# Turning the feed-forward hidden blocks with 32x32 transposes on VectorE and DMAs, in place of 128x128 transposes on TensorE

## The chip, the cores and the metric

The kernel runs on one core of a Trainium2 chip. The metric is device time in microseconds (us) for one execution; smaller is better. The core's engines run side by side and wait for one another through semaphores: TensorE (PE; its weight loads are shown apart as PEld), VectorE (DVE), ScalarE (ACT), GpSimd (POOL) and SyncE (SP), which issues nearly all DMAs. An "engine queue" below is the fixed order in which one engine takes its instructions: what stands behind a waiting instruction waits too.

## What is computed

One encoder layer on a sequence of 256 tokens of width 2048, all in float32: a feed-forward half step, a mixer (a gated linear recurrence beside a windowed attention), and a second feed-forward half step, each closed by a layer norm. Only the two feed-forward steps are touched by the change:

```python
def swiglu(x, w_in, w_out):
    gate, up = jnp.split(x @ w_in, 2, axis=-1)
    return (jax.nn.silu(gate) * up) @ w_out
...
h = layer_norm(DEEPNORM_ALPHA * h + 0.5 * swiglu(h, ffn1_w_in[layer], ffn1_w_out[layer]), ...)
mix = hybrid_mixer(h, ...)
h = layer_norm(DEEPNORM_ALPHA * h + mix, ...)
h = layer_norm(DEEPNORM_ALPHA * h + 0.5 * swiglu(h, ffn2_w_in[layer], ffn2_w_out[layer]), ...)
```

The hidden width `D_FF` is 5632, so the hidden activations of one step are 256 x 5632 float32 numbers.

## The kernel before

Every large product is a `Job`: a stretch of columns of one weight matrix, multiplied with the activations of all 256 tokens (two token tiles `t` of 128). Weights stream in from device memory in chunks of 1 MB: 128 partitions x `RAW` = 2048 numbers, loaded by one DMA of SP into a buffer `raw` (L165; three buffers). To keep float32 precision, each half of a chunk (128 x 1024) is split in two parts: ACT rounds it to `wH` (a cast), DVE subtracts that from the original and gets the rest `wL` (both L182; four buffers of each). TensorE then does three products per weight tile, `xH*wH`, `xH*wL` and `xL*wH` (L235), where `xH`, `xL` are the two parts of the activations.

The feed-forward step (`ffn`, L390) walks over the hidden columns in blocks: one of 512 columns, then five of 1024. For each block there is a gate job (its result goes through the sigmoid on ACT, L400, and a product on DVE, L401), an up job (multiplied in by DVE, L405), and two output jobs (`outs`), which multiply the finished hidden block with `w_out` and add into `acc` (L426). The order of jobs is: gate and up of block b, then the two output jobs of block b-1, and so on; at the end the output jobs of the last two blocks follow each other. Steps of a job are one chunk long.

The hidden block comes out with tokens on the partitions, as `silu` (128 tokens x 2 x 1024). The output jobs need hidden columns on the partitions, as `hH` and `hL`. So `hid` (L407) appends a generator to the list `fast`, and `pump` (L147) lets it advance after each weight chunk, by a budget. Before the change the generator calls `to_x2` (L305) per 512 columns: eight 128x128 transposes on TensorE (L109, against the identity, into two banks of PSUM called `tp`), and for each bank a split: a cast on ACT to `hH` (L115) and a subtraction on DVE to `hL` (L116). `ready` (L419) makes the program wait, in its order of writing, for a block's turn to be complete ahead of its output jobs. The final order on each engine is made by the framework's scheduler from this program and from priorities.

The last output job of a step takes two `silu` buffers as weight buffers (`room`, L441), once they are free.

Of the kernel before, what the change touches and what calls it, by code (L numbers as in the profile page):

```python
# [10 lines left out]
F32 = mybir.dt.float32  # L11
# [6 lines left out]
P = 128  # L18
SEQ = 256
NT = SEQ // P  # L20
# [50 lines left out]
def kernel(ctx, tc, x, ffn1_in, ffn1_out, ln1_g, ln1_b, mix_in, lb_fwd, lb_bwd,  # L71
                             norm_g, w_a, w_b, mix_out, ln2_g, ln2_b, ffn2_in, ffn2_out, ln3_g,
                             ln3_b, hmask_d, amask_d, rope_d, out):
    nc = tc.nc
    x, out = x[0], out[0]
# [29 lines left out]
    turned = []  # L105

    def transpose4(srcs):
        ps = tp_tile()
        turned[:] = [nc.tensor.transpose(out=ps[:, i * P:(i + 1) * P], in_=s, identity=ident)  # L109
                     for i, s in enumerate(srcs)]  # L110
        return ps

    def split(ps, H, L):

        nc.scalar.copy(out=H, in_=ps)  # L115
        return nc.vector.tensor_sub(out=L, in0=ps, in1=H.bitcast(F32))  # L116
# [23 lines left out]
    def step(q):  # L140
        try:
            return next(q[0]) or 0.3
        except StopIteration:
            q.pop(0)
            return 0.0
# [159 lines left out]
    def to_x2(src, xo, c):  # L305

        ps = []
        for t in range(NT):
            ps.append(transpose4([src(t)[:, i * P:(i + 1) * P] for i in range(4)]))
            if t == 0 and burst:  # L310
                tc.add_manual_dep(turned[0].ins, burst[0].ins.name, NOSYNC, reason="not until both banks are free")
        for t in range(NT):
            ts = slice(t * P, (t + 1) * P)
            burst[:] = [split(ps[t].rearrange("p (k s) -> p k s", k=4), xo[0][:, 4 * c:4 * c + 4, ts],
                              xo[1][:, 4 * c:4 * c + 4, ts])]


    stats = {}

    def acc_stats(t, c):  # L320
        if t not in stats:
            stats[t] = small.tile([P, 4, 6], F32, tag=f"st{t}", name="st")
        nc.vector.bn_stats(stats[t][:, c, :], acc[:, t, c * 512:(c + 1) * 512])  # L323
# [66 lines left out]
    def ffn(w_in, w_out, cur, pool, before, tpost, post, hook):  # L390
        blocks = [(0, 512)] + [(c, 1024) for c in range(512, DFF, 1024)]
        jobs, outs = [], []
        for bi, (c0, C) in enumerate(blocks):
            st = {}

            def gate(t, j, ps, st=st, C=C):
                if "s" not in st:
                    st["s"] = pool().tile([P, NT, 1024], F32, tag="silu", name="silu", bufs=2)
                s = st["s"][:, t, j * 512:(j + 1) * 512]
                nc.scalar.activation(out=s, in_=ps, func=AF.Sigmoid)  # L400
                nc.vector.tensor_mul(s, s, ps)  # L401

            def up(t, j, ps, st=st):
                s = st["s"][:, t, j * 512:(j + 1) * 512]
                nc.vector.tensor_mul(s, s, ps)  # L405

            def hid(st=st, C=C):  # L407
                st["H"] = pool().tile([P, 8, SEQ], F32R, tag="hH", name="hH", bufs=2)
                st["L"] = pool().tile([P, 8, SEQ], F32R, tag="hL", name="hL", bufs=2)

                def gen():
                    yield 2.6
                    for c in range(C // 512):
                        to_x2(lambda t: st["s"][:, t, c * 512:(c + 1) * 512], (st["H"], st["L"]), c)
                        yield 2.6
                    st["turned"] = True
                fast.append(gen())

            def ready(st=st):  # L419
                while "turned" not in st:  # L420
                    step(fast)

            def oevac(half, last):
                def f(t, j, ps):
                    a = acc[:, t, half * 1024 + j * 512:half * 1024 + (j + 1) * 512]
                    nc.vector.scalar_tensor_tensor(a, ps, 0.5, a, op0=OP.mult, op1=OP.add)  # L426
                    if last:
                        acc_stats(t, half * 2 + j)
                return f

            last = bi == len(blocks) - 1
            jobs.append(Job(w_in, 0, KD, c0, C, lambda: cur["x"], gate))
            jobs.append(Job(w_in, 0, KD, DFF + c0, C, lambda: cur["x"], up, post=hid))
            ob = [Job(w_out, c0 // P, C // P, h * 1024, 1024, lambda st=st: (st["H"], st["L"]), oevac(h, last),
                      pre=ready if h == 0 else None) for h in range(2)]
            outs.append(ob)
            if bi > 0:
                jobs += outs[bi - 1]
        outs[-2][0].pre = lambda pre=outs[-2][0].pre: (pre(), before())
        jobs += outs[-1]  # L440
        def room(r):  # L441
            if r < 2:
                return None
            return [pool().tile([P, RAW], F32R, tag=("early", "silu")[r - 2], name="early", bufs=2) for _ in range(2)]

        jobs[0].head = 2
        last = jobs[-1]
        last.tail, last.room, last.tpost, last.post, last.hook = 4, room, tpost, post, hook
        return jobs
# [313 lines left out]
    for g in range(4):  # L763
        st = {}
# [302 lines left out]
```

## Time and profile before

| what | value |
|---|---|
| median of 3 runs | 2590.62 us (2590.59 to 2590.93) |
| the profiled execution: its own time, its span | 2590.6 us, 2588.7 us |
| mean granted TensorE clock | 0.999 |
| ScalarE busy | 1165.0 us (45%) |
| GpSimd busy | 4.8 us |
| moved by DMA | 483.22 MB, mean 187 GB/s |

The span runs from the first to the last instruction; 1.9 us of the measured time lie outside it. In the rows shown below, a timeline row is: start (us from the span's start), duration (us), engine, line of the kernel, operation, output<-inputs, shape, how many instructions were merged into the row, and in square brackets how long the engine was idle before and whose instruction ended that. A row of a group is: line, engine, operation, names, shapes, count, then after the bar the summed busy time (us) and the mean duration of one (ns), then the engine's idle time ahead of them. Rows for "SPq" are DMA issues on SP's queue.

### The profile page before, as it was taken

Reading aid. Unit: us, or ns where it says so; the run is one execution under the profiler, and the core shown is the slowest. Engines: PE = TensorE matmul, PEld = TensorE weight load, DVE = VectorE, ACT = ScalarE, POOL = GpSimd, SP = SyncE. Lnnn points to the kernel's source line nnn. Section 1 sums busy time; section 2 is a strip of 40 time slices with the busy share of each in tenths; the row PEclk is TensorE's granted clock in tenths of the full one; section 3 lists DMA queues with packets and bytes.
Section 4 is the critical chain, followed back from the end, with each engine's and each line's share of the span. In section 5 each row is a group of like instructions: output and inputs, shape, how many; then the busy total and the mean of one; then the engine's idle time right before and its main releaser. Section 6 shows DMA issues by size and latency. Waiting matters only on the chain.

```text
span 2588.7 us, 30175 instructions
## 1 busy us (share of the span) xinstructions
PE 2570.8 (99%) x12141; PEld 2145.6 (83%) x12141; DVE 1546.8 (60%) x1919; ACT 1165.0 (45%) x1449; POOL 4.8 (0%) x28
## 2 busy tenths in 40 slices
PE   9999999999999999999999999999999999999998
PEld 7888888888878888888888888888788888888886
DVE  5455555454586888877544544556755455555557
ACT  5444444444445455554544544444544444444442
POOL 0000000000000000000000000000000000000000
PEclk9999999999999999999999999999999999999999
DMA  7555555555655554554555455556555555555563
GB/s 252 191 194 186 190 195 191 191 187 195 221 171 194 167 175 147 178 164 156 191 185 188 137 179 195 196 185 221 175 185 193 195 186 191 192 195 183 192 226 130
DMA packets 147307, 483.22 MB, mean 187 GB/s; under 512 B 7696, under 2 KB 7904, under 8 KB 146400
## 3 DMA queue, kind: packets, MB, share of 16 engines
q1 hardware_dynamic: 145712, 473.99, 55.0%
q10 hardware_dynamic: 1456, 7.32, 0.7%
q8 instruction: 95, 1.56, 0.2%
q14 instruction: 44, 0.36, 0.0%
HBM read 479.17 MB, written 2.10 MB: 186 GB/s over the span
## 4 chain that ended last, share of the span: by engine, by line
PE 97%; DVE 2%; DMA 1%; issue 0%; SPq 0%; DVEq 0%; ACT 0%; ACTq 0%
PE ps L235 82%; PE ps L254 10%; PE tp L109 2%; PE tp L710 1%; PE tp L714 1%; DVE wL L182 0%; DVE lnu L343 0%; DMA raw<-in_ffn_w_in 0%; PE tp L744 0%; DVE lnu L347 0%; PE tp L876 0%; PE tp L741 0%; PE tp L729 0%; PE tp L884 0%; DVE st L323 0%; DMA acc<-in_x 0%
## 5 line engine op out<-in xcount | busy, mean ns | idle before, releaser
L182 DVE TENSOR_TENSOR wL<-raw,wH 128x1024 fp32r<-128x1024 f32 (+1 forms) x890 | 1076.5, 1216 | 976.6 <-ACT wH L182 966.7
L182 ACT CAST wH<-raw 128x1024 fp32r<-128x1024 f32 (+1 forms) x890 | 927.6, 1047 | 1235.8 <-PE ps L235 1147.3
L235 PE MATMUL ps<-wH,xHL 128*128 128x512 f32 x4672 | 1286.8, 390 | 2.8 <-ACT xHL L115 1.7
L235 PEld LDWEIGHTS ps<-wH,xHL 128*128 128x128 f32 x4672 | 875.4, 188 | 184.7 <-ACT xHL L115 2.8
L235 PE MATMUL ps<-wL,xHL 128*128 128x512 f32 x2336 | 746.3, 390 | 0.0
L235 PEld LDWEIGHTS ps<-wL,xHL 128*128 128x128 f32 x2336 | 438.2, 188 | 90.0
L235 PE MATMUL ps<-wH,hH 128*128 128x512 f32 x672 | 208.8, 392 | 0.0
L235 PE MATMUL ps<-wH,hL 128*128 128x512 f32 x672 | 207.0, 389 | 0.0
L235 PE MATMUL ps<-wL,hH 128*128 128x512 f32 x672 | 206.9, 389 | 0.0
L254 PE MATMUL ps<-xHL,wH 128*128 128x512 f32 x768 | 195.5, 394 | 0.0
L254 PEld LDWEIGHTS ps<-xHL,wH 128*128 128x128 f32 x768 | 137.6, 189 | 24.2
L235 PEld LDWEIGHTS ps<-wL,hH 128*128 128x128 f32 x672 | 126.1, 188 | 26.3
L235 PEld LDWEIGHTS ps<-wH,hL 128*128 128x128 f32 x672 | 126.1, 188 | 26.3
L235 PEld LDWEIGHTS ps<-wH,hH 128*128 128x128 f32 x672 | 124.7, 188 | 24.7
L254 PEld LDWEIGHTS ps<-xHL,wL 128*128 128x128 f32 x768 | 104.6, 190 | 7.3
L254 PE MATMUL ps<-xHL,wL 128*128 128x256 f32 x768 | 107.3, 283 | 0.0
L426 DVE SCALAR_TENSOR_TENSOR acc<-ps,acc 128x512 f32<-128x512 f32 x96 | 60.3, 682 | 0.7 <-PE ps L235 0.6
L235 PE MATMUL ps<-wH,zH 128*128 128x512 f32 x112 | 34.8, 390 | 0.0
L235 PE MATMUL ps<-wH,zL 128*128 128x512 f32 x112 | 34.7, 390 | 0.0
L235 PE MATMUL ps<-wL,zH 128*128 128x512 f32 x112 | 34.7, 391 | 0.0
L116 DVE TENSOR_TENSOR hL<-tp,hH 128x512 fp32r<-128x512 f32 x44 | 28.2, 683 | 6.8 <-ACT hH L115 6.8
L657 DVE RECIPROCAL wqr<-we 128x256 f32<-128x256 f32 x16 | 28.0, 1750 | 1.8 <-PE tp L710 1.8
(183 smaller groups left out, 1149.6 us busy)
## 6 DMA issues: line engine op xcount, KB each, us to landing
raw<-in_ffn_w_in SPq DMA_DIRECT2D x173, 1024.0 KB, 4.9
raw<-in_mix_w_in SPq DMA_DIRECT2D x148, 1024.0 KB, 4.9
raw<-in_ffn_w_out SPq DMA_DIRECT2D x88, 1024.0 KB, 5.0
raw<-in_w_branch_a SPq DMA_DIRECT2D x16, 1024.0 KB, 5.0
raw<-in_mix_w_out SPq DMA_DIRECT2D x16, 1024.0 KB, 5.2
raw<-in_w_branch_b SPq DMA_DIRECT2D x4, 1024.0 KB, 4.9
raw<-in_ffn_w_in SPq DMA_DIRECT2D x6, 512.0 KB, 6.7
gbt<-in_ln_g ACTq DMA_DIRECT2D x3, 1024.0 KB, 5.0
```

What stands on the lines that cost most here:

```text
L109: turned[:] = [nc.tensor.transpose(out=ps[:, i * P:(i + 1) * P], in_=s, identity=ident) for i, s in enumerate(srcs)]
L116: return nc.vector.tensor_sub(out=L, in0=ps, in1=H.bitcast(F32))
L182: both = nc.scalar.copy(out=H[:, c], in_=s[:, c]), nc.vector.tensor_sub(out=L[:, c], in0=s[:, c], in1=H[:, c].bitcast(F32))
L235: one = nc.tensor.matmul(out=job.ps[t, j], lhsT=job.lhs(a, k, t, j), rhs=b[:, o + j * 512:o + (j + 1) * 512], start=first, stop=last)
L254: nc.tensor.matmul(out=job.ps[h][:, 0:cols], lhsT=w[:, o + h * P:o + (h + 1) * P], rhs=xHL[:, k, 0:cols], start=k == 0 and part == 0, stop ...
L426: nc.vector.scalar_tensor_tensor(a, ps, 0.5, a, op0=OP.mult, op1=OP.add)
L657: nc.vector.reciprocal(r[:, 0:256], ex[:, 0:256])
L710: nc.tensor.matmul(out=pa[:, (d * NT + t) * P:(d * NT + t + 1) * P], lhsT=tok(KS[d], h, t), rhs=tok(QR[d], h, t), start=True, stop=True)
L714: nc.tensor.matmul(out=pc[:, (i * NT + t) * P:(i * NT + t + 1) * P], lhsT=tok(a, h, t), rhs=tok(b, h, t), start=True, stop=True)
```

## The change

A new helper `turn` replaces `to_x2` in the feed-forward generator; `to_x2` stays for the mixer. For a block of `nk` x 128 hidden columns (`nk` is 4 or 8):

- DVE transposes each token tile of `silu` (128 x 512 or 128 x 1024) in 32x32 blocks into a new buffer `turn`, one instruction per token tile. Inside each band of 32 partitions the blocks are then turned, but a band of 32 tokens still sits on its own 32 partitions.
- Sixteen DMAs on SP's queue carry band `i`, group `q` to the partitions `32*q` of the buffer `turned` (`raw` in the code; it shares the rotating buffers of the tag `silu`). Each moves 32 partitions x 512 numbers (64 KB), or 32 x 2 x 128 numbers in the first block.
- The split reads `turned` instead of PSUM: one cast on ACT (L115) and one subtraction on DVE (L116) for each token tile, on 128 x 8 x 128 numbers, where before there were two of each on 128 x 4 x 128.

The builder's argument `dynamic_dma_scratch_size` sets how many bytes of each SBUF partition are reserved for the descriptors that GpSimd would write; its default is 16384, and 4096 leaves room for `turn`. GpSimd issues no DMA in either kernel. Lines behind the new function move by 20 to 22.

```diff
+    Q = P // 32
+
+    def turn(src, nk, pool, tag, xo, k0=0):
+        tt = pool.tile([P, Q, NT, 8, 32], F32, tag="turn", name="turn")
+        for t in range(NT):
+            nc.vector.transpose(out=tt[:, :, t, 0:nk].rearrange("p q k b -> p k q b"), in_=src(t))
+            yield 1.3
+        yield 2.6
+        raw = pool.tile([P, Q, NT, 8, 32], F32, tag=tag, name="turned", bufs=2)
+        for i in range(Q):
+            for q in range(Q):
+                nc.sync.dma_start(out=raw[32 * q:32 * (q + 1), i, :, 0:nk], in_=tt[32 * i:32 * (i + 1), q, :, 0:nk])
+            yield 1.3
+        yield 2.6
+        for t in range(NT):
+            ts = slice(t * P, (t + 1) * P)
+            split(raw[:, :, t, 0:nk].rearrange("p i k b -> p k i b"),
+                  *(a[:, k0:k0 + nk, ts].rearrange("p k (i b) -> p k i b", i=Q) for a in xo))
+            yield 2.6
@@ def gen():
                     yield 2.6
-                    for c in range(C // 512):
-                        to_x2(lambda t: st["s"][:, t, c * 512:(c + 1) * 512], (st["H"], st["L"]), c)
-                        yield 2.6
+                    yield from turn(lambda t: st["s"][:, t, 0:C], C // P, pool(), "silu", (st["H"], st["L"]))
                     st["turned"] = True
@@ def kernel(**inputs):
-    nc = _bacc.Bacc("TRN2", target_bir_lowering=False, num_devices=1)
+    nc = _bacc.Bacc("TRN2", target_bir_lowering=False, num_devices=1, dynamic_dma_scratch_size=4096)
```

On TensorE the order of all other instructions is the same; only the 176 rows `tp<-ident,silu` are gone. Three other engines are shown, around the turn of the third block (1024 columns) of the first step. In each row stands the line, the operation, the names and one operand's shape; rows that follow each other alike are counted.

SP's queue of DMAs before, from the up and gate loads of the second block to the gate and up loads of the fourth (`raw` is a weight chunk):

```order
L165 DMA raw<-in_ffn_w_in 128x2x1024 x16
L165 DMA raw<-in_ffn_w_out 128x2x1024 x4
L165 DMA raw<-in_ffn_w_in 128x2x1024 x16
L165 DMA raw<-in_ffn_w_out 128x2x1024 x8
L165 DMA raw<-in_ffn_w_in 128x2x1024 x16
```

And now, from the output loads of the first block on (the first `turned` row here belongs to the second block, the next to the third):

```order
L165 DMA raw<-in_ffn_w_out 128x2x1024 x4
L165 DMA raw<-in_ffn_w_in 128x2x1024
L330 DMA turned<-turn 32x512 x16
L165 DMA raw<-in_ffn_w_in 128x2x1024 x15
L165 DMA raw<-in_ffn_w_out 128x2x1024 x5
L330 DMA turned<-turn 32x512 x16
L165 DMA raw<-in_ffn_w_out 128x2x1024 x3
```

Sixteen small DMAs now stand between the fifth and the sixth chunk that follow a block's up job. The same place with what each row waits for (eight semaphores `DMAHW0` to `DMAHW7` are given to SP's DMAs in turn, so that a DMA waits for the one eight places ahead of it; `DVE` is the semaphore of VectorE; the number behind the underscore is a label):

```order
L330 DMA turned<-turn 32x512 [waits DMAHW4_49]
L330 DMA turned<-turn 32x512 [waits DMAHW5_49]
L330 DMA turned<-turn 32x512 [waits DMAHW6_49]
L330 DMA turned<-turn 32x512 [waits DMAHW7_49]
L330 DMA turned<-turn 32x512 [waits DMAHW0_49]
L330 DMA turned<-turn 32x512 [waits DMAHW1_49]
L165 DMA raw<-in_ffn_w_out 128x2x1024 [waits DMAHW2_49,DVE_49]
L165 DMA raw<-in_ffn_w_out 128x2x1024 [waits DMAHW3_49,DVE_49]
```

The first of the sixteen waits for DVE, the last eight each for the landing of one of the first eight, and the next weight loads each for one of the last eight.

DVE before, from the up product of the third block (`silu<-silu,ps`) to the evacuation of the second block's last output job (`acc<-ps,acc`):

```order
L405 TENSOR_TENSOR silu<-silu,ps 128x512 x4
L182 TENSOR_TENSOR wL<-raw,wH 128x1024 x3
L116 TENSOR_TENSOR hL<-tp,hH 128x4x128 x2
L182 TENSOR_TENSOR wL<-raw,wH 128x1024 x2
L116 TENSOR_TENSOR hL<-tp,hH 128x4x128 x2
L182 TENSOR_TENSOR wL<-raw,wH 128x1024 x3
L426 SCALAR_TENSOR_TENSOR acc<-ps,acc 128x512 x4
L182 TENSOR_TENSOR wL<-raw,wH 128x1024 x8
L426 SCALAR_TENSOR_TENSOR acc<-ps,acc 128x512 x4
```

And now:

```order
L427 TENSOR_TENSOR silu<-silu,ps 128x512 x4
L182 TENSOR_TENSOR wL<-raw,wH 128x1024
L324 STREAM_TRANSPOSE turn<-silu 128x8x4x32 x2
L182 TENSOR_TENSOR wL<-raw,wH 128x1024 x6
L446 SCALAR_TENSOR_TENSOR acc<-ps,acc 128x512 x4
L116 TENSOR_TENSOR hL<-turned,hH 128x8x128 x2
L182 TENSOR_TENSOR wL<-raw,wH 128x1024 x9
L446 SCALAR_TENSOR_TENSOR acc<-ps,acc 128x512 x4
```

The two transposes come one weight half after the up product, and the split moved from the third and fifth weight half behind the up product to behind the first evacuation of `acc`.

ACT before, from the sigmoid of the third block's gate to the casts of the next block:

```order
L400 ACTIVATE silu<-ps 128x512 x4
L182 CAST wH<-raw 128x1024 x19
L115 CAST hH<-tp 128x4x128 x2
L182 CAST wH<-raw 128x1024 x2
L115 CAST hH<-tp 128x4x128 x2
L182 CAST wH<-raw 128x1024 x27
```

And now:

```order
L422 ACTIVATE silu<-ps 128x512 x4
L182 CAST wH<-raw 128x1024 x23
L115 CAST hH<-turned 128x8x128 x2
L182 CAST wH<-raw 128x1024 x25
L422 ACTIVATE silu<-ps 128x512 x4
```

The cast of the split now stands two to four weight halves later, right behind both halves of the weight chunk whose load is the last ahead of the sixteen DMAs.

## The prediction

> **What bounds the kernel now.** I read the page's head first, then the chain of work that ended last, then the groups of TensorE with shapes kept apart.
>
> ```profile
> span 2588.7 us, 30175 instructions
> PE 2570.8 (99%) x12141; PEld 2145.6 (83%) x12141; DVE 1546.8 (60%) x1919; ACT 1165.0 (45%) x1449; POOL 4.8 (0%) x28
> ...
> PE 97%; DVE 2%; DMA 1%; issue 0%; SPq 0%; DVEq 0%; ACT 0%; ACTq 0%
> ```
>
> TensorE is busy 99% of the span and makes 97% of the chain, so whatever leaves its stream shortens the run as long as it keeps being fed. What the change takes from it is one row of its groups:
>
> ```profile
> L109 PE MATMUL tp<-ident,silu 128*128 128x128 f32 x176 | 22.8, 272 | 0.0
> ```
>
> 176 transposes in 22 groups of eight. The busy column (22.8 us) counts overlapping ends, so I price a group by what it does to the stream. TensorE's timeline in the third block:
>
> ```profile
> 257.83 0.62 PE L235 MATMUL ps<-wH,hL 128*128 128x512 f32 x2
> 258.29 1.03 PE L109 MATMUL tp<-ident,silu 128*128 128x128 f32 x8
> 259.08 0.71 PE L235 MATMUL ps<-wH,hH 128*128 128x512 f32 x2
> 259.63 0.62 PE L235 MATMUL ps<-wL,hH 128*128 128x512 f32 x2
> 260.09 0.62 PE L235 MATMUL ps<-wH,hL 128*128 128x512 f32 x2
> ```
>
> A pair of products goes by every 0.46 us (259.63 to 260.09). From 258.29 to 259.63 lie one pair and the eight transposes: 1.34 - 0.46 = 0.88 us. ACT's timeline at the same place says it once more, since its casts wait for TensorE to free a buffer:
>
> ```profile
> 255.77 1.05 ACT L182 CAST wH<-raw 128x1024 fp32r<-128x1024 f32 x1 [1.66 <-PE ps L235]
> 258.49 1.05 ACT L182 CAST wH<-raw 128x1024 fp32r<-128x1024 f32 x1 [1.67 <-PE ps L235]
> 259.44 1.07 ACT L115 CAST hH<-tp 128x512 fp32r<-128x512 f32 x2
> 262.10 1.05 ACT L182 CAST wH<-raw 128x1024 fp32r<-128x1024 f32 x1 [1.59 <-PE ps L235]
> ```
>
> A weight half normally takes 2.72 us (255.77 to 258.49); the one with a group in it takes 3.61 (to 262.10), 0.89 more. **Removed: 22 x 0.89 = 19.6 us.** The matmuls that stay keep their order, so nothing is given back on TensorE itself. The question is whether its feeding, which now has three new kinds of work in its queues, stays hidden.
>
> **VectorE's transposes.** The trace of before holds no such operation. The nearest rows are DVE's groups on float32 from SBUF:
>
> ```profile
> L182 DVE TENSOR_TENSOR wL<-raw,wH 128x1024 fp32r<-128x1024 f32 x878 | 1068.8, 1223 | 975.7 <-ACT wH L182 966.0 <-PE ps L254 9.4
> L116 DVE TENSOR_TENSOR hL<-tp,hH 128x512 fp32r<-128x512 f32 x44 | 28.2, 683 | 6.8 <-ACT hH L115 6.8
> L657 DVE RECIPROCAL wqr<-we 128x256 f32<-128x256 f32 x16 | 28.0, 1750 | 1.8 <-PE tp L710 1.8
> ```
>
> A 128 x 1024 subtraction takes 1.22 us; the slowest elementwise row, the reciprocal, would take 4 x 1.75 = 7.0 us for 1024 numbers. I take 1.2 us, because a transpose reads and writes each number once as the subtraction does, and keep 7.0 as the other end. Where it falls, from DVE's timeline:
>
> ```profile
> 252.56 2.47 DVE L405 TENSOR_TENSOR silu<-silu,ps 128x512 f32<-128x512 f32 x4
> 254.95 1.22 DVE L182 TENSOR_TENSOR wL<-raw,wH 128x1024 fp32r<-128x1024 f32 x1
> 256.85 1.23 DVE L182 TENSOR_TENSOR wL<-raw,wH 128x1024 fp32r<-128x1024 f32 x1 [0.69 <-ACT wH L182]
> 259.57 1.23 DVE L182 TENSOR_TENSOR wL<-raw,wH 128x1024 fp32r<-128x1024 f32 x1 [1.49 <-ACT wH L182]
> ...
> 276.10 2.48 DVE L426 SCALAR_TENSOR_TENSOR acc<-ps,acc 128x512 f32<-128x512 f32 x4
> ```
>
> The two transposes start at 256.17, when the subtraction of 254.95 ends, and hold back the one of 256.85 until 258.6. Queued behind is `wL`, for which TensorE waits. That half was cast from 255.77 on, when TensorE freed its slot; with four slots it is used three halves later, at 255.77 + 8.16 = 263.9, its `wL` one pair of products later, at 264.4. So the two transposes may take 264.4 - 1.23 - 256.17 = 7.0 us together before TensorE waits; 2.4 are spent. Later subtractions come every 2.72 us and take 1.23, so DVE catches up within two halves. Price: nothing, hidden by 4.6 us of buffered weights; without that cover 2.4 us in each of ten blocks.
>
> The Trainium skill speaks against this step (VectorE: DVE Perf Modes, "Rules for kernel authors"): a 128x128 transpose belongs on TensorE where PSUM will do. Its table there gives 311 ns for VectorE on 128x128 bf16, by which eight of them make an estimated 2.5 us, 5.0 for the pair; the sum would be the same. No row here shows a VectorE transpose.
>
> **The split** becomes two subtractions of 1.22 us behind the evacuation at 276.10, in place of four of 0.68 at two earlier places. Behind `acc` the next subtraction starts at about 281.0 instead of 278.6; its half is used near 285. Hidden. On ACT two casts of 128 x 1024 at 1.05 replace four that take 1.07 a pair: equal work.
>
> **The sixteen DMAs** move through SP's queue, ahead of weight loads. SP's timeline in two windows, and the issues with their time to landing:
>
> ```profile
> 244.51 0.37 SPq L165 DMA_DIRECT2D raw<-in_ffn_w_out  x1
> 249.95 0.37 SPq L165 DMA_DIRECT2D raw<-in_ffn_w_out  x1
> ```
>
> ```profile
> raw<-in_ffn_w_out SPq DMA_DIRECT2D x88, 1024.0 KB, 5.0
> acc<-in_x SPq DMA_DIRECT2D x8, 256.0 KB, 7.3
> out<-lnu SPq DMA_DIRECT2D x8, 256.0 KB, 2.0
> ```
>
> One issue costs SP 0.37 us. A load goes out as soon as the second subtraction of the buffer's old chunk ends, every 5.44 us; the fifth behind the up job goes at 256.2, then SP waits for the transposes until 258.6, which costs nothing, since the sixth is due only at 260.8. Call R the time from 258.6 until the sixth can go out. Sixteen issues are 16 x 0.37 = 5.9 us. A 64 KB transfer lands after 2.0 (the row of `out`) to 7.3 us (that of `acc`), and only eight are out at a time, so the second eight wait for the first: two rounds of 2.0 fit inside the 5.9, two of 7.3 make 14.6. I take R = 7, near the short end, because the queue is nearly empty at that point: one older load is out, due to land at 261.2.
>
> What R may be: the cast of 255.77 belongs to the third load (out at 244.51), and each load has two casts; without the groups the sixth load's first cast is due six halves later, at 255.77 + 6 x 2.72 = 272.1. With 5.0 us to land the load must go by 267.1, so R = 8.5 costs not even ACT anything. Behind that TensorE still has three halves in hand (8.16 us, and 0.46 more until `wL`): it waits only if the cast starts after 272.1 + 8.6 - 1.05 - 1.23 = 278.4, that is R above 14.8. The split's cast stands on ACT at 270.4, behind the fifth load's second cast; with R = 7 the last band goes out near 265.2 and lands near 267, three us early. Traffic is small: 2 x 5632 x 1024 bytes = 11.5 MB on
>
> ```profile
> q1 hardware_dynamic: 145712, 473.99, 55.0%
> ```
>
> adds 2.4% to a queue that keeps the sixteen DMA engines 55% busy.
>
> **The last block** of a step has the least room, since its output jobs follow soon. DVE's timeline there:
>
> ```profile
> 2487.20 2.48 DVE L405 TENSOR_TENSOR silu<-silu,ps 128x512 f32<-128x512 f32 x4
> ...
> 2532.51 2.48 DVE L426 SCALAR_TENSOR_TENSOR acc<-ps,acc 128x512 f32<-128x512 f32 x4
> ```
>
> Its output jobs begin where the earlier ones end, at 2532.5. The split comes 23.5 us behind the up product (276.10 - 252.56), so at 2510.7 plus 2.5: 19 us early.
>
> **Sum.** 2590.6 (the profiled execution, which is also the median; 1.9 us of it outside the span) - 19.6 + 0 = 2571.0 us.
>
> **Rivals.**
>
> (a) *SP's queue becomes the bound; slower.* Sixteen transfers go out late and the weights behind them starve TensorE. The cost is R - 14.8 us in each of twelve turns; it eats the gain at R = 14.8 + 19.6/12 = 16.4 us. If each transfer had to land before the next (16 x 2.0 = 32 us), it is 12 x 17.2 = 206: 2777 us. For it: every semaphore round on a DMA costs microseconds in the rows above, and loads must queue behind. Against: the same queue keeps several transfers out at once. Chance 6%. The Trainium skill (DMA: Bandwidth & Descriptors, "Measured") gives 0.95 us for a 64 KB transfer and calls what is smaller descriptor-dominated; one after another that is an estimated 15.2 us, 5 us in all, 2576.
>
> (b) *VectorE's transposes are slow; slower.* At the reciprocal's rate the pair takes 14.0 us, TensorE waits 7.0 in each of ten blocks: 2571 + 70 = 2641 us. It decides from 4.5 us each on (7.0 + 1.96 for two). For it: no row shows the operation, and its output is written in runs of 32 numbers. Against: both subtraction rows above stay at 1.2 to 1.3 ns a number in each partition. Chance 4%.
>
> (c) *Partly paid back.* ACT or DVE waits in order for a late band or a late load, and TensorE loses half to one us a turn, 6 to 12 us in all: about 2580. For it: twelve turns put DVE, SP and ACT in a row, each waiting for the one before. Against: the room of 4.6 and 7.8 us worked out above. Chance 12%.
>
> (d) *The gain isn't there:* TensorE waits for something else in the freed time, and the time stays at 2590. Against: the chain is TensorE's own for 97%. Chance 3%.
>
> **How the numbers follow.** The forecast holds 75%. Its own spread is 2567.8 (all 22.8 us of the busy column go) to about 2574. I reach up into (c) as far as 2580, so the range is 2567 to 2580; above it lie (a), (b), (d) and part of (c), some 18%. What can be told from no change is about 0.2%, 5.2 us: faster means below 2585.4. Faster has the forecast and nearly all of (c), 86%; same has (d) and a little of (a) and (c), 5%; slower has the rest, 9%.
>
> **What would show it.** Right: the row `tp<-ident,silu` gone, TensorE 19 to 20 us shorter at 99% busy, ACT's casts in the feed-forward at an even 2.72 us, transposes of 1.1 to 2.5 us, bands landing before the split asks. Wrong: waits of `ps` on `wH` or `wL` right behind each turn, ACT idle ahead of `hH<-turned`, or SP's weight loads bunched up more than 15 us behind the first band.

## The result and the profile after

The changed kernel takes 2570.97 us (median of 4 runs, 2570.86 to 2571.25), the kernel before 2590.61 us (4 runs, 2590.59 to 2590.93): a ratio of 0.9924, 95% interval 0.9907 to 0.9941. It is 19.64 us faster; the forecast was 2571.0 in a range of 2567 to 2580.

The head of the page of after and the shares of its chain:

```profile
span 2569.3 us, 30102 instructions
PE 2552.1 (99%) x11965; PEld 2128.7 (83%) x11965; DVE 1569.0 (61%) x1923; ACT 1164.5 (45%) x1429; POOL 4.8 (0%) x28
...
PE 97%; DVE 2%; DMA 1%; issue 0%; SPq 0%; DVEq 0%; ACT 0%; ACTq 0%
```

The span is 19.4 us shorter and TensorE's busy time 18.7 us (2570.8 - 2552.1), with 176 instructions fewer. Everything else on the chain stayed: TensorE still makes 97% of it. VectorE is busy 22.2 us longer. TensorE's timeline in the third block, at the place where eight transposes had stood (columns as in the prediction's timelines):

```profile
257.71 0.62 PE L235 MATMUL ps<-wL,hH 128*128 128x512 f32 x2
258.16 0.62 PE L235 MATMUL ps<-wH,hL 128*128 128x512 f32 x2
258.62 0.61 PE L235 MATMUL ps<-wH,hH 128*128 128x512 f32 x2
```

A pair every 0.45 to 0.46 us, with nothing between. Now the three engines that took over. VectorE's groups by shape (busy us, mean ns of one, idle before), and its timeline behind the third block's up product:

```profile
L324 DVE STREAM_TRANSPOSE turn<-silu 128x1024 f32<-128x1024 f32 x20 | 23.6, 1220 | 0.0
L116 DVE TENSOR_TENSOR hL<-turned,hH 128x1024 fp32r<-128x1024 f32 x20 | 23.5, 1217 | 0.0
```

```profile
250.17 2.48 DVE L427 TENSOR_TENSOR silu<-silu,ps 128x512 f32<-128x512 f32 x4
252.56 1.22 DVE L182 TENSOR_TENSOR wL<-raw,wH 128x1024 fp32r<-128x1024 f32 x1
253.69 2.36 DVE L324 STREAM_TRANSPOSE turn<-silu 128x1024 f32<-128x1024 f32 x2
255.98 2.43 DVE L182 TENSOR_TENSOR wL<-raw,wH 128x1024 fp32r<-128x1024 f32 x2
...
259.90 1.23 DVE L182 TENSOR_TENSOR wL<-raw,wH 128x1024 fp32r<-128x1024 f32 x1 [1.49 <-ACT wH L182]
...
270.83 2.65 DVE L446 SCALAR_TENSOR_TENSOR acc<-ps,acc 128x512 f32<-128x512 f32 x4 [1.54 <-PE ps L235]
273.40 2.35 DVE L116 TENSOR_TENSOR hL<-turned,hH 128x1024 fp32r<-128x1024 f32 x2
```

The pair of transposes takes 2.36 us, as a pair of subtractions does, the two subtractions behind it run back to back, and the next one waits for ACT again (259.90): VectorE has caught up after two halves. SP's queue around the same turn, the issues of the small DMAs by themselves (min, median and max ns of one, then its time to landing in us), and ACT:

```profile
256.08 10.03 SPq L330 DMA_DIRECT2D turned<-turn  x16
266.21 3.47 SPq L165 DMA_DIRECT2D raw<-in_ffn_w_out  x3
```

```profile
L330 SPq DMA_DIRECT2D turned<-turn x192: 507/589/1253, 58.0 to 2487.2; - x192
...
DMA to landing us min/median/max: 1.8/2.0/6.3
```

```profile
267.93 1.99 ACT L115 CAST hH<-turned 128x1024 fp32r<-128x1024 f32 x2
...
273.02 2.01 ACT L182 CAST wH<-raw 128x1024 fp32r<-128x1024 f32 x2 [3.10 <-DMA raw<-in_ffn_w_out]
275.49 1.06 ACT L182 CAST wH<-raw 128x1024 fp32r<-128x1024 f32 x1 [0.47 <-DMA raw<-in_ffn_w_out]
277.86 1.05 ACT L182 CAST wH<-raw 128x1024 fp32r<-128x1024 f32 x1 [1.30 <-PE ps L235]
```

The sixteen issues hold SP for 10.03 us, 0.63 us each. The sixth load goes out at 266.21, and ACT stands 3.10 us for it. The three casts from then on have one pause between them, 0.47 us for the next load, and behind them ACT waits for TensorE again (277.86): TensorE never ran out of halves. ACT's waits over the whole run (us, times, longest) say how often this happens:

```profile
ACT wH L182 <- DMA raw<-in_ffn_w_out: 17.0, 12, 3.1
...
ACT hH L115 <- DMA turned<-turn: 6.1, 7, 2.4
...
ACT wH L182 <- DMA raw<-in_ffn_w_in: 5.6, 4, 1.9
```

So the change moved 19 us of work off the engine that sets the end, and its waits ended inside ACT's own idle time. TensorE has no wait for `wH` at a turn; its only one, 0.5 us, stands at the start of the program.

### The profile page after: what moved, and what is told of

Its sections match the earlier page's. It is cut to its first block, busy times and chain, and to the rows that moved or that the text cites. A ratio compares the mean times of both kernels' runs of the same rounds, so it can differ in the third digit from the quotient of the medians.

```text
span 2569.3 us, 30102 instructions
## 1 busy us (share of the span) xinstructions
PE 2552.1 (99%) x11965; PEld 2128.7 (83%) x11965; DVE 1569.0 (61%) x1923; ACT 1164.5 (45%) x1429; POOL 4.8 (0%) x28
## 4 chain that ended last, share of the span: by engine, by line
PE 97%; DVE 2%; DMA 1%; issue 0%; SPq 0%; DVEq 0%; ACT 0%; ACTq 0%
PE ps L235 83%; PE ps L254 10%; PE tp L109 1%; PE tp L730 1%; PE tp L734 1%; DVE wL L182 0%; DVE lnu L365 0%; DMA raw<-in_ffn_w_in 0%; PE tp L764 0%; DVE lnu L369 0%; PE tp L896 0%; PE tp L761 0%; PE tp L749 0%; PE tp L904 0%; DVE st L345 0%; DMA acc<-in_x 0%
## 5 line engine op out<-in xcount | busy, mean ns | idle before, releaser
L423 DVE TENSOR_TENSOR silu<-silu,ps 128x512 f32<-128x512 f32 x44 | 27.3, 681 | 0.7 <-ACT silu L422 0.7
```

## The experiments

All times are device us, all ratios against the kernel before, run beside each kernel. "Theory" is that of the prediction: TensorE's stream sets the end, everything new is hidden by limits that can be reached. The changes are against the kernel after, except where said.

**The reservation alone** (before, with the new argument):

```diff
-    nc = _bacc.Bacc("TRN2", target_bir_lowering=False, num_devices=1)
+    nc = _bacc.Bacc("TRN2", target_bir_lowering=False, num_devices=1, dynamic_dma_scratch_size=4096)
```

> The kernel before with nothing but the smaller reservation (4096 bytes in place of 16384), so all tiles lie at other addresses; the TensorE transposes stay. Theory (all of the gain is TensorE's stream, 22 groups of 0.89 us): 2590.6 us, no change. Rival (part of the gain comes from where the tiles lie): between 2571 and 2590, say 2580.

2590.82 us, ratio 1.0001 (0.9992 to 1.001). The argument and the buffers' new places have no part in the gain.

**Both ways at once.** The new turn stays, and TensorE makes its old transposes too, whose results nobody reads:

```diff
             nc.vector.transpose(out=tt[:, :, t, 0:nk].rearrange("p q k b -> p k q b"), in_=src(t))
+            for c in range(nk // 4):
+                transpose4([src(t)[:, c * 512 + i * P:c * 512 + (i + 1) * P] for i in range(4)])
```

> The changed kernel with the 176 TensorE transposes put back into PSUM banks that nobody reads; the new way still makes the result. Theory: they cost what they cost before, 176 x 0.10 + about 0.1 for each run of them, 18.5 to 19.6 us, so 2589.5 to 2590.6 us. Rival (the gain came from the changed work on ACT and DVE or from the order, and TensorE would have absorbed the transposes): 2571.

2590.34 us, ratio 0.9999 (0.999 to 1.0009). The group is back on TensorE:

```profile
L109 PE MATMUL tp<-ident,silu 128*128 128x128 f32 x176 | 21.1, 272 | 0.0
```

All of the gain is given back by TensorE's 176 transposes alone, with the move of the split, the DMAs and VectorE's work left as in after.

**No turn at all.** The split reads the hidden block as it is; this leaves the turning out, and the output products get the block unturned:

```diff
-                    yield from turn(lambda t: st["s"][:, t, 0:C], C // P, pool(), "silu", (st["H"], st["L"]))
+                    for t in range(NT):
+                        ts = slice(t * P, (t + 1) * P)
+                        split(st["s"][:, t, 0:C].rearrange("p (k s) -> p k s", s=P),
+                              st["H"][:, 0:C // P, ts], st["L"][:, 0:C // P, ts])
+                        yield 2.6
```

> The changed kernel without any turn: no VectorE transposes, no small DMAs; the splits read the hidden block as it lies, so the hidden block enters the output products unturned. Theory (the new way is wholly hidden): 2571.0 us, within 0.5 of the changed kernel. Rival (it costs a little in each of twelve turns): 2566 to 2569.

2571.28 us, ratio 0.9925 (0.991 to 0.994). Without VectorE's transposes and without the DMAs it is no faster than with them: the new way costs nothing that can be measured. With the run before it, this brackets the sum: 19.6 us come off, and nothing is paid.

**VectorE's limit: each transpose made twice, then four times**

```diff
-            nc.vector.transpose(out=tt[:, :, t, 0:nk].rearrange("p q k b -> p k q b"), in_=src(t))
+            for _ in range(2):    # and 4
+                nc.vector.transpose(out=tt[:, :, t, 0:nk].rearrange("p q k b -> p k q b"), in_=src(t))
```

> The changed kernel with each VectorE transpose made twice: the pair takes 4.7 us instead of 2.4. Theory (hidden by buffered weights: the next wL may end 2.4 us later still, the sixth weight load lands 0.7 us ahead of its limit): 2571 us. Rival (VectorE's time in a turn is on the path): 20 x 1.2 = 24 us more, 2595.

> Each VectorE transpose made four times: the pair takes 9.4 us, 7.1 more than in the changed kernel. Theory: the next wL ends 2.3 us too late, and the sixth weight load, which goes out behind DMAs that waited for the transposes, lands 4.0 us too late; the two overlap, so 4.0 us in each of ten turns: 2611 us (2594 if only the wL counts, 2571 + 10 x 2.3). Rival (on the path in full): 20 x 3.5 = 71 us, 2642. Rival (never on the path): 2571.

Twice: 2571.91 us, ratio 0.9927 (0.9912 to 0.9942), no different from after though VectorE is busy 24.4 us longer. Four times: 2609.59 us, ratio 1.0073 (1.0058 to 1.0088). The third block's turn with four, in VectorE's timeline, TensorE's, and TensorE's waits:

```profile
256.12 9.12 DVE L325 STREAM_TRANSPOSE turn<-silu 128x1024 f32<-128x1024 f32 x8
```

```profile
266.40 0.73 PE L235 MATMUL ps<-wL,hH 128*128 128x512 f32 x2 [1.57 <-DVE wL L182]
...
283.21 1.20 PE L235 MATMUL ps<-wH,hH 128*128 128x512 f32 x4 [1.08 <-ACT wH L182]
```

```profile
PE ps L235 <- DVE wL L182: 16.6, 10, 2.0
...
PE ps L235 <- ACT wH L182: 10.9, 9, 2.1
```

The theory's limit for the pair was 7.0 us, so 9.12 us should leave TensorE without `wL` for 2.1 us; it waits 1.57. The limit is thus 7.5 us here, and after spends 2.36 of it. The total comes near the expected one by another route than was written: the wait for `wL` and the later one for the delayed weight loads don't overlap, they stand 17 us apart and add up (27.5 us in all, of which 0.4 stand at the start of the program), and 11.2 us more are spent in slower products (PE busy 2563.3 against 2552.1).

**SP's limit: the small DMAs doubled, at half the size, and every second one cut**

```diff
-                nc.sync.dma_start(out=raw[32 * q:32 * (q + 1), i, :, 0:nk], in_=tt[32 * i:32 * (i + 1), q, :, 0:nk])
+                for t in range(NT):
+                    nc.sync.dma_start(out=raw[32 * q:32 * (q + 1), i, t, 0:nk], in_=tt[32 * i:32 * (i + 1), q, t, 0:nk])
```

That makes 32 DMAs a turn; for 24 the added lines are:

```diff
+                for ts in ((slice(0, NT),) if q % 2 else (slice(0, 1), slice(1, NT))):
+                    nc.sync.dma_start(out=raw[32 * q:32 * (q + 1), i, ts, 0:nk], in_=tt[32 * i:32 * (i + 1), q, ts, 0:nk])
```

> Each of the small DMAs cut in two (one per token tile): 32 a turn, the same bytes. In the changed kernel one such issue takes SP 0.63 us (16 in 10.0 us), and the sixth weight load lands 6.8 us after it goes out, 3.0 us before TensorE would have to wait. Theory (the cover is that size and SP's issue time is what fills it): the sixth load goes out 10.1 us later, TensorE waits 10.1 - 3.0 = 7.1 us in each of ten to twelve turns, 71 to 85 us: about 2645 us (2625 to 2660), with waits of ps on wH or wL behind each turn. Rival (bytes or landing set the time in SP's queue, not the number of issues): the turn stays near 10 us and the time at 2571.

> 24 small DMAs a turn (every second one cut in two by token tile). At 0.64 us each SP's queue is taken for 15.4 us. The run with 32 DMAs was blocked for 20.0 us and TensorE waited 5.6 us a turn, so the cover ends at about 14.4 us. Theory (the cover is a fixed room, and a pause of TensorE of about one us leaves the granted clock at 1.00, as the pauses of 1.1 and 1.6 us in the run with four transposes did): waits of 1.0 us in ten to twelve turns and nothing more, 2581 to 2583 us. Rival (the price of a late load grows in proportion to the number of DMAs beyond sixteen, 95 us for sixteen more): 2571 + 48 = 2619.

With 32 issues: 2666.09 us (2664.42 to 2667.61), ratio 1.0291 (1.0276 to 1.0307), a little over the expected range. SP, then TensorE, in the third block:

```profile
266.36 20.68 SPq L331 DMA_DIRECT2D turned<-turn  x32
287.45 1.39 SPq L165 DMA_DIRECT2D raw<-in_ffn_w_out  x3
```

```profile
288.61 0.61 PE L235 MATMUL ps<-wH,hL 128*128 128x512 f32 x2
295.05 2.08 PE L235 MATMUL ps<-wH,hH 128*128 128x512 f32 x4 [5.83 <-ACT wH L182]
296.93 1.05 PE L235 MATMUL ps<-wL,hH 128*128 128x512 f32 x2
```

The same bytes in twice the issues hold SP twice as long, so SP pays by the issue and not by the byte. Nor do the pieces of a DMA set it: in the first block of the kernel after, a DMA has two runs of 128 numbers in each partition instead of one of 512, and sixteen still hold SP for 10.40 us. Counted from the end of the transposes (267.46 here), R is 20.0 us and the wait 5.83: the cover is 14.2 us, against 14.8 in the prediction. The twelve waits of the run, from 1.76 to 8.82 us, sum to 67.7 us, and 24.4 us more of the 93.2 by which the span grew stand in PE's busy time (2576.5): after each pause TensorE runs slowly for a while. The stretches before, in and behind the pause, by the view of windows (stretch, us, busy us of PE, PEld, DVE, ACT and POOL with counts, granted clock, DMA share, GB/s):

```profile
280.00:291.00 11.00, 9.22 (x41) 7.32 (x39) 5.52 (x7) 2.00 (x2) 0.00 (x0) 1.00 0.37 99
291.00:297.00 6.00, 1.95 (x5) 1.57 (x6) 2.08 (x3) 2.56 (x3) 0.00 (x0) 0.80 0.96 377
297.00:303.00 6.00, 6.00 (x26) 4.94 (x25) 3.98 (x4) 3.32 (x4) 0.00 (x0) 0.92 0.87 307
```

The four products behind the pause take 2.08 us, where 1.20 us is the row of four behind a short pause in the four-transposes run above, and the granted clock is below 1 in both later windows. The Trainium skill (TensorE: Matmul & The Clock Gate, "What's actually happening") has TensorE fall to half rate after an idle window of some 3.4 us; the rows agree for the pauses of 3.75 us and more. Shorter ones can do it too: in this run the two shortest, 2.38 and 1.76 us, are followed by slow products as well. The shortest:

```profile
1958.40 1.19 PE L235 MATMUL ps<-wH,xHL 128*128 128x512 f32 x4 [1.76 <-ACT wH L182]
...
1961.05 1.05 PE L235 MATMUL ps<-wL,xHL 128*128 128x512 f32 x2
```

A pair takes 0.62 us at full rate, and the granted clock is 0.76 from 1958.4 to 1962.0. So the idle window of that page is not the limit here.

With 24 issues: 2595.05 us (2593.34 to 2597.06), ratio 1.0016 (1.0007 to 1.0025), between the theory and its rival. SP in the third block, then four of TensorE's eight waits at turns, two in the middle of a step and the last block of each step:

```profile
254.99 15.57 SPq L331 DMA_DIRECT2D turned<-turn  x24
270.66 1.58 SPq L165 DMA_DIRECT2D raw<-in_ffn_w_out  x3
```

```profile
278.44 1.20 PE L235 MATMUL ps<-wH,hH 128*128 128x512 f32 x4 [0.60 <-ACT wH L182]
...
411.48 1.20 PE L235 MATMUL ps<-wH,hH 128*128 128x512 f32 x4 [1.81 <-ACT wH L182]
...
678.24 2.08 PE L235 MATMUL ps<-wH,hH 128*128 128x512 f32 x4 [3.75 <-ACT wH L182]
...
2518.64 2.07 PE L235 MATMUL ps<-wH,hH 128*128 128x512 f32 x4 [4.48 <-ACT wH L182]
```

In the third block the transposes end at 256.09, so R is 14.6 us, and the wait is 0.60: a cover of 14.0 us, as with 32. The eight waits sum to 14.8 us, and PE's busy time is 8.0 us longer than in the kernel after. The last blocks wait far longer than the rest, which the theory did not have. SP's turn takes 18.69 and 18.46 us there instead of 15.57, since in each of them one small DMA waits for the weight load eight places ahead (SP's waits: us, times, longest):

```profile
SPq L331 <- DMA raw<-in_ffn_w_out: 5.5, 2, 3.0
```

Those loads land 8.2 and 8.3 us after they go out, where 5.1 is the median. Two 1 MB loads of the layer norm's constants are under way on ACT's queue at that time, but that they made the weights late was not tried.

**Another queue for the small DMAs: GpSimd's**

```diff
-                nc.sync.dma_start(out=raw[32 * q:32 * (q + 1), i, :, 0:nk], in_=tt[32 * i:32 * (i + 1), q, :, 0:nk])
+                nc.gpsimd.dma_start(out=raw[32 * q:32 * (q + 1), i, :, 0:nk], in_=tt[32 * i:32 * (i + 1), q, :, 0:nk])
```

> The sixteen DMAs are issued from GpSimd's queue, which has nothing else to do in these stages, instead of SP's. Theory (SP's delay is hidden): the time stays at 2571.0 us, while ACT's waits of wH for raw loads, 17.0 and 5.6 us in the changed kernel, fall to about 1. Rival (SP's delay costs something): 2566 to 2570.

2571.47 us, ratio 0.9926 (0.9909 to 0.9942): the same as after. The weight loads no longer queue behind the turn, and ACT's waits for them are gone but for 1.3 us, yet nothing is gained, because those waits cost TensorE nothing; nor do ACT's waits for the bands, which rise from 6.1 to 22.7 us. The small DMAs have a price of their own there, in the issues (KB each, median us from issue to landing) and in the issue's own time:

```profile
turned<-turn POOLq DMA_DIRECT2D x160, 64.0 KB, 5.6
```

```profile
L330 POOL DMA_DIRECT2D turned<-turn x192: 496/496/679, 57.8 to 2486.8; - x192
```

**Why an issue takes 0.59 us.** The small DMAs touch 32 partitions and have both ends in the chip's own memory. Here the weight loads are cut into four of 32 partitions, to see whether the partitions make it:

```diff
-            nc.sync.dma_start(out=raw[:, q * job.C:(q + kp) * job.C].rearrange("p (k c) -> p k c", k=kp),
-                              in_=job.w[r0:r0 + kp * P, job.c0:job.c0 + job.C].rearrange("(k p) c -> p k c", p=P))
+            for b in range(0, P, 32 if parts == 1 else P):
+                e = b + (32 if parts == 1 else P)
+                nc.sync.dma_start(out=raw[b:e, q * job.C:(q + kp) * job.C].rearrange("p (k c) -> p k c", k=kp),
+                                  in_=job.w[r0:r0 + kp * P, job.c0:job.c0 + job.C].rearrange("(k p) c -> p k c", p=P)[b:e])
```

> The changed kernel with each weight load cut into four DMAs of 32 partitions (4 x 256 KB), to see what makes an issue of the turn's DMAs take SP 0.59 to 0.63 us where a weight load takes 0.37. If it is the 32 partitions, these issues take 0.6 us as well; if it is that source and destination both lie in SBUF, they stay at 0.37. The time: 2571 to 2580, since four issues of 0.6 fit in 5.44 us but come on top of the turn's ten.

3014.52 us in one run: the expectation of the time was missed by far. The question itself is answered by one row (min, median and max ns of an issue):

```profile
L167 SPq DMA_DIRECT2D raw<-in_ffn_w_out x352: 311/426/1697, 132.3 to 2972.2; - x176
```

From 0.31 us (a load ahead of which SP had paused) on, with a median of 0.43 (one right behind another), is near the 0.37 us of a whole load and below 0.59: the 32 partitions don't make the long issue. What does is open; that both ends lie in the chip was not tried by itself. Why the whole run grew by more than 400 us is not settled either. TensorE waits 223 us for `wH` and `wL` there, and its busy time is 154 us longer, so the weights came late. Each load now waits for the one eight places ahead, which is two chunks earlier instead of eight, and the engines' order changed with it.

**Further on the same way: the mixer's `oA`.** Its 32 transposes per run on TensorE become two turns of 1024 columns (with a reservation of 256 bytes to make room), ACT's scaled copies reading the turned buffer:

```diff
-                ps = transpose4([oA[:, 2 * h2 + h, t, :] for h in range(2) for t in range(NT)])
...
+                    nc.vector.transpose(out=tt[:, :, t].rearrange("p q k b -> p k q b"),
+                                        in_=oA[:, 8 * h8:8 * h8 + 8, t, :].rearrange("p k (q b) -> p k q b", b=32))
...
+                        nc.sync.dma_start(out=raw[32 * q:32 * (q + 1), i], in_=tt[32 * i:32 * (i + 1), q])
...
+                    nc.scalar.activation(out=oA[:, hd].rearrange("p t (i b) -> p t i b", b=32),
+                                         in_=raw[:, :, :, k, :].rearrange("p i t b -> p t i b"), func=AF.Copy,
                                          scale=ngT[:, hd:hd + 1])
```

> The changed kernel with a further 32 TensorE transposes, those of the recurrence's output oA, done the new way (two turns of 1024 columns, result scaled on ACT as before; the reservation goes down to 256 bytes to make room). Theory (a group of eight is worth 0.89 us wherever TensorE is the bound and the turn isn't asked for at once): 4 x 0.89 = 3.6 us less, 2567.4 us. Rival (in that stage ACT or SP has less room, two turns stall): 2571 to 2580.

2569.23 us (2568.68 to 2570.06), ratio 0.9917 (0.9902 to 0.9932). It is the fastest kernel of this study by its median, but 1.7 us under after is less than these intervals tell apart. Part of the expected 3.6 us went into one wait (TensorE's row, then ACT's, then TensorE's transposes of `ast`, a tile of the attention with three buffers):

```profile
1287.26 1.19 PE L235 MATMUL ps<-wH,xHL 128*128 128x512 f32 x4 [1.62 <-ACT wH L182]
```

```profile
1276.07 2.51 ACT L838 ACTIVATE oA<-turned,ngT 128x256 f32<-128x256 f32 x6
1285.28 0.58 ACT L867 COPY ast<-ps 128x512 f32<-128x512 f32 x1 [6.71 <-issue]
```

```profile
1284.60 1.03 PE L109 MATMUL tp<-ident,ast 128*128 128x128 f32 x8
```

It is not the scaled copies' own time: six of them end at 1278.58. ACT then stands idle for 6.71 us ahead of the copy into `ast`, whose semaphore wait ends when the first of TensorE's transposes of `ast` are done, and the cast that TensorE needs stands behind that copy. In the kernel after, four of those transposes come at 1278.69, and the copy starts without a wait at 1279.39. The generators in `fast` are served in turn, so the turn of `oA`, which stands ahead in that list, puts these transposes off. That is read from the trace and the code; no run tried it by itself.

The last try spreads the scaled copies: four turns of 512 columns, with all small DMAs on GpSimd's queue.

```diff
+            for h4 in range(4):
+                tt = p.tile([P, Q, NT, 4, 32], F32, tag="turn", name="turn")
...
+                        nc.gpsimd.dma_start(out=raw[32 * q:32 * (q + 1), i], in_=tt[32 * i:32 * (i + 1), q])
+                    yield 2.6
...
-                yield 0.3
+                    yield 1.3
```

> All small DMAs on GpSimd's queue, and the 32 transposes of oA done the new way in four turns of 512 columns, with ACT's scaled copies spread between its weight casts. Theory (the run with two turns of 1024 columns lost 1.6 of its 3.6 us to one wait of TensorE behind eight ACT copies in a row, at 1287 us): without that wait 2571.2 - 3.6 = 2567.5 us. Rival (that stage has no room for the new way whatever its queue): 2569 or more.

2576.6 us (2575.29 to 2580.0), ratio 0.9947 (0.9931 to 0.9964): the rival won. The longest waits of TensorE in that stage:

```profile
1274.24 0.73 PE L235 MATMUL ps<-wL,xHL 128*128 128x512 f32 x2 [1.66 <-DVE wL L182]
...
1289.80 0.73 PE L235 MATMUL ps<-wH,xHL 128*128 128x512 f32 x2 [2.11 <-ACT wH L182]
```

Once VectorE holds `wL` back and once ACT `wH`; all waits of the stage sum to about 5.5 us. Right ahead of these rows ACT and VectorE stand still themselves, for bands on GpSimd's queue (us, times, longest):

```profile
ACT oA L838 <- DMA turned<-turn: 29.8, 4, 9.0
DVE turn L826 <- DMA turned<-turn: 19.0, 3, 8.0
```

A cast or a subtraction of a weight half that stands behind such a wait comes late. In both tries, then, it is the order within ACT's and VectorE's queues that costs. This try changed the spreading and the queue together, so which of the two made it slower is not shown.

## Why the prediction was right, point by point

- **Removed, 22 x 0.89 = 19.6 us: right.** 19.64 us in the medians. The runs with both ways and with no turn show that it is TensorE's stream and that nothing else is in the sum. The price of a group in the stream was the right number to take: the group's busy column (22.8 us) would have been 3 us too much.
- **VectorE's transposes at 1.2 us, bounds 1.2 to 7.0: right.** 1.18 us by the pair, 1.22 us by the group's mean. The limit of 7.0 us for the pair measured 7.5. In rival (b) the mechanism exists, as the run with four transposes shows; its premise, slow transposes, did not hold.
- **R = 7: mis-sized.** R is 10.2 us (256.05 to 266.21). The landing of 2.0 us held; the issue's price did not: the prediction took the 0.37 us of a weight load, and an issue between two places in the chip's memory takes 0.59, 0.63 with what lies between. Sixteen of them are 10 us, not 5.9. The row of a 1 MB load that goes out by itself was the wrong neighbour for the issue; a small part of the difference is that the small DMAs follow each other without a pause (the first, at 256.08, takes 0.51).
- **The sixth load's landing, 5.0 us: too short.** It takes 6.8 (266.21 to 273.02), with two more held-back loads right behind it. So ACT waits 3.10 us; the prediction had it wait from R = 8.5 on, and R went past that.
- **The cover of 14.8: right to 0.7 us.** 14.2 us with 32 issues, 14.0 with 24. Two errors nearly cancel in it: the landing was 1.8 us too short, and the working let TensorE wait for `wL` (1.23 - 0.46 us more) where the rows name the cast of `wH`; 14.8 - 1.8 + 0.8 = 13.8. That it came out so near was luck. The wrong R cost nothing because the cover is wider still: it ate room, not time. Of the cover 14.1 - 10.2 = 3.9 us were left, not 7.8, so rival (a) was nearer than the prediction's room made it look. With 24 issues instead of 16 the whole gain is lost.
- **The prices behind the limits: too low.** Rival (a) counted R - 14.8 per turn and no more. The 32-issue run paid 67.7 us in waits, near 12 x (20.0 - 14.8) = 62, and another 24.4 in slow products. By the working of rival (b) the four transposes would cost 10 x (9.12 - 7.0) = 21 us; they cost 38.6, since the late weight loads and slower products come on top.
- **The bands three us early: wrong, and free.** ACT waits for `turned` in 7 of the turns, 6.1 us in all, since the last band goes out 3 us later. This is the same mis-sized issue. ACT idle ahead of `hH<-turned` was named as a sign that the forecast is wrong; it came, and the forecast held, because ACT had the time.
- **The split and the last block: right.** The split runs behind `acc`'s evacuation, 2.35 us, and TensorE waits for it nowhere.
- **A sign that was wrong:** ACT's casts at an even 2.72 us. They bunch behind each turn (the rows at 273.02 and 275.49) while TensorE runs evenly. TensorE's pitch, not ACT's, shows whether a feed holds.

## What to carry to other kernels

When one engine makes 97% of the chain, price what leaves it by the pitch of its stream, and price what replaces it by room: how long each queue may be blocked before the buffered work runs out. The small DMAs here cost their queue the same time at 64 and at 32 KB, so count the issues and find their price for the same two ends before trusting the margin; here sixteen fitted and twenty-four did not. Where other work waits in the same queues the same change may not pay: in the mixer weight casts came late behind instructions that waited, and nothing more was gained that could be told.

## What the runs showed of the hardware that was not expected

- **The issue of a small DMA is dearer than that of a large one.** 0.59 us for 64 KB between two places in the chip's memory, against 0.37 us for a 1 MB weight load that goes out by itself (0.42 to 0.44 in the median right behind another), and halving the bytes leaves it so (32 issues in 20.68 us). On GpSimd's queue the issue takes 0.50 us, but the same transfer lands after 5.6 us instead of 2.0.
- **A pause of TensorE can cost more than itself.** In the run with four transposes, pauses up to 1.8 us left the clock at 1.00, and of the three slightly over 2 us two were followed by about 3.4 us at half rate and one was not. In the 32-issue run slow products follow all twelve pauses, from 1.76 us on, and cost about 2 us a pause (24.4 us in all). Behind pauses of 3.75 us and more four products take 1.61 to 2.08 instead of 1.20 us. What decides for a pause of about 2 us is open.
- **VectorE turns 128x1024 float32 numbers in 32x32 blocks as fast as it subtracts them,** 1.22 us each. The estimate of 2.5 us that the prediction worked out from the Trainium skill (VectorE: DVE Perf Modes, "The three transpose paths") is twice the measured time.
